# A hybrid attention, RG-LRU and conformer trunk whose own scheduler is given other durations for its matmuls

## The chip, the cores and the metric

The kernel runs on one core of a Trainium2 chip. The metric is the device time of one execution in microseconds (us). The core's engines are TensorE (PE in the profile; its weight loads are shown apart as PEld), VectorE (DVE), ScalarE (ACT), GpSimd (POOL) and SyncE (SP), which here only issues transfers (DMAs).

## The reference

Two layers of this, for 256 tokens of width 1024, all in float32 (cut; `causal_dwconv`, `banded_causal_attention` and the norms are left out):

```python
h = rms_norm(x, norm_mix_pre[l])
proj = h @ w_in[l]
q, k, v, lru_x, lru_gate, glu_in, gate_logits = jnp.split(proj, IN_SPLITS, axis=-1)
y_a = dilated_attention_mixer(q, k, v, cos, sin, w_o_attn[l])   # 3 groups of 8 heads of 64
y_b = rg_lru_mixer(lru_x, lru_gate, ...)                        # causal conv, gates, associative scan
y_c = conformer_conv_mixer(glu_in, ...)   # GLU, 31-tap causal conv, LayerNorm over 1024 channels
g = jax.nn.sigmoid(gate_logits).reshape(B, S, N_BRANCHES, D)
merged = g[:, :, 0] * y_a + g[:, :, 1] * y_b + g[:, :, 2] * y_c
x = x + rms_norm(merged @ w_out[l], norm_mix_post[l])
h = rms_norm(x, norm_mlp_pre[l])
u = jnp.square(jax.nn.relu(h @ w_mlp_up[l]))                    # 1024 -> 4096
x = x + rms_norm(u @ w_mlp_down[l], norm_mlp_post[l])
```

## The kernel before

**Weights.** The weight matrices come from HBM as 184 chunks of 128 x 2048 float32 (1 MB), each by one DMA that SP issues (tiles `raw_*`, two buffers). ACT casts each chunk to a shorter format (`whi_*`, two casts of 128 x 1024, line 416), DVE subtracts that from the chunk and keeps the rest (`wlo_*`, two subtractions, line 429), and PE multiplies in three passes: activations high and low (`hh`, `hl`) with `whi`, and activations high with `wlo`. A chunk gives 48 matmuls of 256 columns, or 24 of 512. They are the main matmuls. In names such as `wlo_gb1_1` the last digit is the layer (0 or 1); `q`, `k`, `v` are the attention's projections, `gb`, `ga`, `gc` the branch gates, `lx`, `lg`, `glu` the inputs of the other two branches, `ob` the output of the RG-LRU, `up` and `dn` the MLP.

**Beside the main matmuls** run: the rotary embedding on DVE (`r1q`, `r2q`, `r1k`, `r2k`); DMAs of 32 KB that copy its result, head by head, into `qk<head pair><group>`, eight per tile, four issued by SP and four by POOL; the scores `sc<head pair><token parity>` on PE, 12 float32 matmuls into the only `sc` buffer; two DVE reductions for each (`sm`, with the row maxima `mx`, line 969), the softmax on ACT, transposes (`tp`) and the products with v on PE; the 31 taps of the conformer conv, some as multiply-adds on DVE (`c`, 128 x 256, line 433), some as products on ACT (`cpd`, line 423) that DVE adds up in a tree of 1024, 512 and 256 columns (`cpd<-cpd`, line 429); the gates' merges (`mg`); the LayerNorm, whose sums over channels are float32 matmuls (`channel_sum`).

**The order.** The kernel doesn't write out its instructions in the order of the source. Each helper (`matmuls`, `tt`, `stt`, `act`, `dma`) makes an operation with an engine, a cost in ns, and what it reads and writes, and `Sched.run` plays a list schedule with these costs: whenever an engine is free in that play, it gets the ready operation with the longest path behind it, by the costs and a table of latencies. The order in which operations were given out is the order in which they are emitted, on all five queues. At run time each engine takes its queue strictly in that order and waits for semaphores, so that a wrong cost doesn't make an operation slow; it changes what stands ahead of what. The main matmuls are tied to each other in the sequence of the list `ORDER`

```python
ORDER = """
    v0 lx1 glu0 glu2 glu3 glu1 glu4 lx0 glu5 glu6 glu7 lx3 lx2 lw0 lw1 lw3 lg1 lg2 lw2 lg0 lg3 q10
    k00 k10 q00 q20 k20 gb0 ob0 gb2 gb1 q11 ob1 gb3 q01 ob3 ob2 ga1 k01 v2 k11 k21 q21 v1 ga0 ga2
    ga3 gc1 gc2 gc0 gc3 oa0 oa1 oc0 oc2 oc1 oc3
""".split()
```

so only the other PE work (scores, transposes, channel sums) can move between them, and so can everything on the other engines. A score operation needs the `sc` buffer free, that is both reductions of the score operation before.

Of the kernel before, what the change touches and what calls it, by code (L numbers as in the profile page):

```python
# [8 lines left out]
F32R = mybir.dt.float32r  # L9
# [367 lines left out]
def trunk_kernel(ctx: ExitStack, tc: tile.TileContext, x_d, pos_d, w_d, lruw_d, par_d, gain_d, const_d, id_d, out_d):  # L377
# [10 lines left out]
    def slot(name, dt=F32, shape=(P, 2, T)):  # L388
        return S.buf(sp, shape, dt, "s2", name, NSLOT)

    def mm_ps(name, shape=(P, 2, T), ring=True):
        return S.buf(pp, shape, F32, "mm", name, 4, ring)
# [4 lines left out]
    def stat(name):  # L397
        return S.buf(sp, (P, 1), F32, "st", name, 32)
# [12 lines left out]
    def act(out, in_, func, scale=1.0, bias=0.0, accum=None):  # L411
        cost = 0.833 * in_.n + (51 if in_.psum else 93) + 93 * aps(scale, bias) + (95 if accum else 0)

        def fn():
            if func is AF.Copy and not isinstance(scale, View) and scale == 1.0:
                nc.scalar.copy(out.ap(), in_.ap())  # L416
                return
            kw = {}
            if isinstance(bias, View) or bias != 0.0:
                kw["bias"] = val(bias)  # L420
            if accum is not None:
                kw["accum_out"] = accum.ap()
            nc.scalar.activation(out.ap(), in_.ap(), func, scale=val(scale), **kw)  # L423

        return S.op("ACT", cost, fn, [in_] + views(scale, bias), [out] + views(accum), TABLE.get(func))
# [19 lines left out]
    def recip(out, a):  # L445
        return S.op("DVE", 8.3 * out.n + 68, lambda: nc.vector.reciprocal(out=out.ap(), in_=a.ap()), [a], [out])

    def dma(eng, out, in_, nbytes):
        def fn():
            o = out.ap() if isinstance(out, View) else out  # L450
            i = in_.ap() if isinstance(in_, View) else in_
            eng.dma_start(out=o, in_=i)

        e = {id(nc.gpsimd): "POOL", id(nc.scalar): "ACT"}.get(id(eng), "SP")
        o = S.op(e, DMA_ISSUE[e], fn, views(in_), views(out))
        o.dma = nbytes / DMA_RATE / 1e3
        return o
# [4 lines left out]
    def matmuls(items):  # L462
        cost = 0
        reads, writes, seen = [], [], set()
        for out, lhs, rhs, start, stop in items:
            n = rhs.n
            cost += n * 0.4266 if lhs.buf.dt == F32R else n * 1.69
            for v, l in ((lhs, reads), (rhs, reads), (out, writes)):
                k = (id(v.buf), v.reg, l is writes)
                if k not in seen:  # L470
                    seen.add(k)
                    l.append(v)

        def fn():
            for out, lhs, rhs, start, stop in items:
                nc.tensor.matmul(out.ap(), lhsT=lhs.ap(), rhs=rhs.ap(), start=start, stop=stop)  # L476

        return S.op("PE", cost, fn, reads, writes)
# [10 lines left out]
    def main(items, *more):  # L489
        for it in (items,) + more:  # L490
            o = matmuls(it)
            o.main = True
            if last_main[0] is not None:
                S.follow(last_main[0], o)
            last_main[0] = o
        return o
# [146 lines left out]
    def add_residual(t, c, m, r):  # L643
# [5 lines left out]
    o = dma(nc.sync, x_sb[:, 0, :], x_d[0:P, :], D * P * 4)  # L649
# [3 lines left out]
                    2048 * P))  # L653
    g_rest = mm_ps("g_rest", (P, 512), False)
    matmuls([(g_rest.all(), unit[0:1, :], g_row[0:1, 512:1024], True, True)])
    S.follow(o, dma(nc.sync, ident.all(), id_d, P * P * 4))
    x1_load = dma(nc.sync, x_sb[:, 1, :], x_d[P:T, :], D * P * 4)
# [82 lines left out]
    for l in range(L):  # L740
# [212 lines left out]
        score_ops = []  # L953

        def scores(hp, t):
            ps = S.buf(pp, (P, 2, 512), F32, "sc", f"sc{hp}{t}_{l}", 1)
            own = slice(t, T, 2)
            it = []
            for g, c, n, ks in ((0, 0, 256, slice(0, T)), (1, 256, P, own), (2, 384, P, own)):
                for e in range(2):  # L960
                    q, rows = qk[hp, g], slice(64 * e, 64 * e + 64)
                    it.append((ps[:, e, c:c + n], q[rows, 0, own], q[rows, 1, ks], True, True))
            score_ops.append(matmuls(it))
            for e in range(2):
                hd = 2 * hp + e
                sb = S.buf(sp, (P, 512), F32, "sm", f"sm{hd}{t}_{l}", NSM)
                s = sb.all()
                mx, nm, ls, rl = (stat(f"{n}{hd}{t}_{l}") for n in ("mx", "nm", "ls", "rl"))
                S.op("DVE", 1.042 * 512 + 76, lambda s=s, mx=mx, e=e: nc.vector.tensor_tensor_reduce(
                    out=s.ap(), in0=ps[:, e, :].ap(), in1=mask[t].ap(), scale=1.0, scalar=-3.0e38, op0=OP.add,  # L970
                    op1=OP.max, accum_out=mx.all().ap()), [ps[:, e, :], mask[t]], [s, mx.all()])
                S.op("ACT", 94, lambda mx=mx, nm=nm: nc.scalar.mul(nm.all().ap(), mx.all().ap(), -0.125),
                     [mx.all()], [nm.all()])
                act(s, s, AF.Exp, scale=0.125, bias=nm.all(), accum=ls.all())
                recip(rl.all(), ls.all())
                act(s, s, AF.Copy, scale=rl.all())
                sm[hd, t] = sb
# [55 lines left out]
        def channel_sum(src, name):  # L1033
            part = mm_ps(f"{name}p_{l}", (P, T), False)
            for r in range(2):
                o = matmuls([(part[32 * c:32 * c + 32, :], ones[:, 0:32], src(4 * r + c), r == 0, r == 1)
                             for c in range(4)])
                o.cost *= 0.14
            sb = slot(f"{name}s_{l}", shape=(P, T))
            act(sb.all(), part.all(), AF.Copy, scale=1.0 / 32)  # L1040
            return sb

        def layer_norm():
            mu = mm_ps(f"mu_{l}", (P, T), False)
            matmuls([(mu.all(), ones.all(), channel_sum(lambda i: cacc[i // 2][:, i % 2, :], "mu").all(), True, True)])
            mub = mu.all().map(lambda a: a[:, None, :].to_broadcast([P, 2, T]))
            sqs = {}
            for j in range(4):
                tt(cacc[j].all(), cacc[j].all(), mub, OP.subtract)
                sqs[j] = slot(f"csq{j}_{l}")  # L1050
                act(sqs[j].all(), cacc[j].all(), AF.Square)
            vs = channel_sum(lambda i: sqs[i // 2][:, i % 2, :], "var")
            var = mm_ps(f"var_{l}", (P, 2), False)
            matmuls([(var[:, t:t + 1], vs[:, t * P:(t + 1) * P], ones[:, 0:1], True, True) for t in range(2)])
# [22 lines left out]
        def attention():  # L1077
            for hp in range(4):
                for t in range(2):
                    scores(hp, t)  # L1080
                for e in range(2):
                    for t in range(2):
                        p_transposes(2 * hp + e, t)
                pv(hp)
# [259 lines left out]
```

## Time and profile before

| what | value |
|---|---|
| median of 3 runs | 1123.21 us (1122.27, 1123.21, 1128.92) |
| the profiled execution | 1124.8 us |
| its span in the trace | 1123.0 us |
| mean granted clock of PE | 0.998 |
| PE busy | 1103.7 us, 98% of the span |
| PE weight loads busy | 1027.6 us, 92% |
| DVE, ACT, POOL busy | 903.7, 726.0, 70.8 us |

Costs are worked out in the trace of the profiled execution, whose own time is 1.6 us above the median; 1.8 us of it lie outside the span. A duration in the rows is that of one instruction from its start to its modelled end; several in a row overlap at their ends, so the step from one to the next is shorter than the duration.

### The profile page before, as it was taken

The numbers are of one execution on the slowest core, as the hardware profiler recorded it, in microseconds if no ns is written. First come the engines' busy times: TensorE is split into PE (matmuls) and PEld (weight loads), VectorE is DVE, ScalarE is ACT, GpSimd is POOL, SyncE is SP. The second block draws the span as 40 slices with busy tenths as digits, with TensorE's granted clock in tenths as the row PEclk, the third lists the DMA queues.
The fourth block names the chain that finished last, engine by engine and source line by source line (L and its number), as shares of the span: only waits on it lengthen the run. The fifth ranks groups of instructions, "written<-read, shape, count | busy, mean of one in ns | idle before, by whom it ended". The sixth has DMA issues, their size and how long they took to land.

```text
span 1123.0 us, 20583 instructions
## 1 busy us (share of the span) xinstructions
PE 1103.7 (98%) x8258; PEld 1027.6 (92%) x8258; DVE 903.7 (80%) x1380; ACT 726.0 (65%) x1184; POOL 70.8 (6%) x156
## 2 busy tenths in 40 slices
PE   7999998999999999999999999999999999999997
PEld 6999998999999889988889999989989998988996
DVE  6999999999969875555679999999997789655554
ACT  5879938588765554444569897469766656444443
POOL 1000021111000010000000000221200001000000
PEclk9999999999999999999999999999999999999999
DMA  8654365655255555555556553765634365655551
GB/s 293 245 208 151 146 219 205 215 165 174 99 186 188 214 199 189 208 193 182 201 188 205 190 179 121 255 216 170 214 124 151 117 240 185 212 192 185 190 203 52
DMA packets 37649, 209.76 MB, mean 187 GB/s; under 512 B 6449, under 2 KB 9777, under 8 KB 14130
## 3 DMA queue, kind: packets, MB, share of 16 engines
q1 hardware_dynamic: 32976, 200.05, 50.7%
q0 software_dynamic: 4576, 8.40, 2.2%
q8 instruction: 65, 1.06, 0.4%
q14 instruction: 30, 0.25, 0.1%
q10 hardware_dynamic: 2, 0.00, 0.0%
HBM read 201.08 MB, written 1.05 MB: 180 GB/s over the span
## 4 chain that ended last, share of the span: by engine, by line
PE 82%; DVE 9%; DMA 4%; ACT 3%; issue 1%; SPq 1%; DVEq 0%; POOL 0%; ACTq 0%
PE dn L476 15%; PE up L476 14%; PE glu L476 8%; PE v L476 5%; PE gc L476 4%; PE wo L476 4%; PE lx L476 4%; PE oc L476 4%; PE lg L476 4%; PE k L476 3%; PE ga L476 3%; PE ob L476 2%; PE ua L476 2%; PE oa L476 2%; PE gb L476 1%; DMA qk<-r1q 1%
## 5 line engine op out<-in xcount | busy, mean ns | idle before, releaser
L429 DVE TENSOR_TENSOR wlo_dn<-raw_dn,whi_dn 128x1024 fp32r<-128x1024 f32 (+1 forms) x66 | 75.8, 1190 | 68.4 <-ACT whi_dn L416 68.4
L416 ACT CAST whi_dn<-raw_dn 128x1024 fp32r<-128x1024 f32 (+1 forms) x66 | 64.4, 1022 | 75.6 <-PE dn L476 44.0
L433 DVE SCALAR_TENSOR_TENSOR c<-upad,parh,c 128x256 f32<-128x256 f32 x256 | 110.5, 479 | 0.1
L476 PE MATMUL up<-hh_mlp,whi_up 128*128 128x256 f32 x448 | 106.3, 278 | 0.0
L476 PE MATMUL up<-hl_mlp,whi_up 128*128 128x256 f32 x448 | 106.0, 278 | 0.0
L476 PE MATMUL dn<-wlo_dn,uh 128*128 128x512 f32 x256 | 100.5, 393 | 0.0
L476 PE MATMUL dn<-whi_dn,uh 128*128 128x512 f32 x256 | 100.4, 392 | 0.0
L429 DVE TENSOR_TENSOR wlo_up<-raw_up,whi_up 128x1024 fp32r<-128x1024 f32 x56 | 66.4, 1222 | 39.1 <-ACT whi_up L416 39.1
L423 ACT ACTIVATE cpd<-upad,parh 128x256 f32<-128x256 f32 x224 | 94.6, 500 | 4.1 <-DVE c L429 4.1
L476 PEld LDWEIGHTS up<-hl_mlp,whi_up 128*128 128x128 f32 x448 | 84.3, 188 | 0.6
L476 PEld LDWEIGHTS up<-hh_mlp,whi_up 128*128 128x128 f32 x448 | 84.2, 188 | 0.6
L416 ACT CAST whi_up<-raw_up 128x1024 fp32r<-128x1024 f32 x56 | 56.2, 1048 | 36.4 <-PE dn L476 17.4
L476 PE MATMUL dn<-whi_dn,ul 128*128 128x512 f32 x256 | 70.8, 392 | 0.0
L429 DVE TENSOR_TENSOR cpd<-cpd 128x1024 f32<-128x1024 f32 (+2 forms) x84 | 63.5, 775 | 0.9 <-ACT cpd L423 0.9
L476 PE MATMUL up<-hh_mlp,wlo_up 128*128 128x256 f32 x448 | 60.7, 278 | 0.0
L476 PE MATMUL glu<-hl_mix,whi_glu 128*128 128x256 f32 x256 | 59.6, 276 | 0.0
L476 PE MATMUL glu<-hh_mix,whi_glu 128*128 128x256 f32 x256 | 59.6, 276 | 0.0
L476 PEld LDWEIGHTS dn<-whi_dn,ul 128*128 128x128 f32 x256 | 48.0, 188 | 10.8
L476 PEld LDWEIGHTS dn<-wlo_dn,uh 128*128 128x128 f32 x256 | 48.0, 188 | 10.3
L476 PEld LDWEIGHTS dn<-whi_dn,uh 128*128 128x128 f32 x256 | 48.1, 188 | 10.3
L476 PEld LDWEIGHTS up<-hh_mlp,wlo_up 128*128 128x128 f32 x448 | 55.7, 188 | 0.0
L476 PEld LDWEIGHTS glu<-hl_mix,whi_glu 128*128 128x128 f32 x256 | 48.0, 188 | 0.0
(309 smaller groups left out, 3388.3 us busy)
## 6 DMA issues: line engine op xcount, KB each, us to landing
raw_dn<-w_in_stream SPq DMA_DIRECT2D x32, 1024.0 KB, 4.8
raw_up<-w_in_stream SPq DMA_DIRECT2D x28, 1024.0 KB, 4.8
raw_glu<-w_in_stream SPq DMA_DIRECT2D x16, 1024.0 KB, 4.9
raw_q<-w_in_stream SPq DMA_DIRECT2D x12, 1024.0 KB, 4.8
raw_k<-w_in_stream SPq DMA_DIRECT2D x12, 1024.0 KB, 4.8
raw_v<-w_in_stream SPq DMA_DIRECT2D x11, 1024.0 KB, 4.9
raw_lx<-w_in_stream SPq DMA_DIRECT2D x8, 1024.0 KB, 4.8
raw_lg<-w_in_stream SPq DMA_DIRECT2D x8, 1024.0 KB, 4.8
```

The lines of the kernel that those rows point to most:

```text
L416: nc.scalar.copy(out.ap(), in_.ap())
L423: nc.scalar.activation(out.ap(), in_.ap(), func, scale=val(scale), **kw)
L429: lambda: nc.vector.tensor_tensor(out=out.ap(), in0=a.ap(), in1=b.ap(), op=op), [a, b], [out])
L433: lambda: nc.vector.scalar_tensor_tensor(out=out.ap(), in0=a.ap(), scalar=val(s), in1=b.ap(), op0=op0, op1=op1), [a, b] + views(s), [out])
L476: nc.tensor.matmul(out.ap(), lhsT=lhs.ap(), rhs=rhs.ap(), start=start, stop=stop)
```

## The change

Three costs that the scheduler plays with are altered; nothing that is computed changes, only the order. A main matmul is taken as 0.446 ns a column where it was 0.4266. Float32 matmuls still cost 1.69 ns a column but at least 180 ns. An operation of the scores is then taken at 0.64 of the sum for its 12 matmuls, and an operation of the channel sums at 0.33 of it where it was 0.14. Below line 963 the changed kernel's lines stand one further down.

```diff
@@ -464,7 +464,7 @@ def matmuls(items):
         for out, lhs, rhs, start, stop in items:
             n = rhs.n
-            cost += n * 0.4266 if lhs.buf.dt == F32R else n * 1.69
+            cost += n * 0.446 if lhs.buf.dt == F32R else max(n * 1.69, 180)
@@ -961,6 +961,7 @@ def scores(hp, t):
             score_ops.append(matmuls(it))
+            score_ops[-1].cost *= 0.64
@@ -1035,7 +1036,7 @@ def channel_sum(src, name):
-                o.cost *= 0.14
+                o.cost *= 0.33
```

The sequence of the main matmuls is the same. On PE, counted in main matmuls of 256 columns, `sc00` keeps its place in both layers, `sc01` of layer 0 moves 24 later, `sc10` 96 earlier in layer 0 and 144 earlier in layer 1 (there it now stands 24 behind `sc01`, which keeps its place), the first transposes 72 to 128 earlier, and the LayerNorm's small products 16 to 232 earlier in layer 0 and up to 24 in layer 1.

DVE, layer 0, from the taps behind the low parts of `wlo_q11` to the second reduction of `sc00`. Before:

```order
L429 TENSOR_TENSOR cpd011_0_1152<-cpd011_0_1152 128x256
L429 TENSOR_TENSOR cpd002_0_1734<-cpd002_0_1734 128x256
L429 TENSOR_TENSOR c0_0_493<-c0_0_493,cpd011_0_1152 128x256
L429 TENSOR_TENSOR wlo_ob1_0_2248<-raw_ob1_0_2153,whi_ob1_0_2216 128x1024 x2
L429 TENSOR_TENSOR c0_0_493<-c0_0_493,cpd002_0_1734 128x256
L433 SCALAR_TENSOR_TENSOR c2_0_786<-upad4_0_85,parh_188,c2_0_786 128x256 x2
L969 ISA sm00_0_2280,mx00_0_2281<-sc00_0_2255,const_261 128x512
L969 ISA mx00_0_2281 128x1
L969 ISA sm10_0_2304,mx10_0_2305<-sc00_0_2255,const_261 128x512
```

After:

```order
L429 TENSOR_TENSOR cpd002_0_1678<-cpd002_0_1678 128x512
L429 TENSOR_TENSOR cpd012_0_1744<-cpd012_0_1744 128x512
L429 TENSOR_TENSOR cpd002_0_1678<-cpd002_0_1678 128x256
L429 TENSOR_TENSOR cpd012_0_1744<-cpd012_0_1744 128x256
L429 TENSOR_TENSOR c0_0_498<-c0_0_498,cpd002_0_1678 128x256
L429 TENSOR_TENSOR c0_0_498<-c0_0_498,cpd012_0_1744 128x256
L429 TENSOR_TENSOR wlo_ob1_0_2268<-raw_ob1_0_2154,whi_ob1_0_2234 128x1024 x2
L433 SCALAR_TENSOR_TENSOR c2_0_791<-upad4_0_85,parh_188,c2_0_791 128x256 x9
L970 ISA sm00_0_2337,mx00_0_2338<-sc00_0_2316,const_261 128x512
L970 ISA mx00_0_2338 128x1
L429 TENSOR_TENSOR wlo_gb3_0_2359<-raw_gb3_0_2229,whi_gb3_0_2323 128x1024 x2
L970 ISA sm10_0_2376,mx10_0_2377<-sc00_0_2316,const_261 128x512
```

Seven more multiply-adds (`c2`) and two tree additions of 512 columns stand ahead of the first reduction, and the two halves of `wlo_gb3` between the first and the second.

SP, layer 1, the transfers issued behind `raw_gb1`. Before:

```order
L452 DMA qk01_1_8282<-r1k10_1_8188 32x256 x2
L452 DMA qk00_1_8354<-r1k00_1_8147 32x256 x2
L452 DMA qk00_1_8354<-r1q00_1_8211 32x256 x2
L452 DMA raw_q11_1_8390<-w_in_stream 128x2048
L452 DMA qk02_1_8395<-r1q20_1_8226 32x256 x2
L452 DMA qk02_1_8395<-r1k20_1_8315 32x256 x2
L452 DMA raw_ob1_1_8433<-w_in_stream 128x2048
L452 DMA raw_gb3_1_8509<-w_in_stream 128x2048
```

After:

```order
L452 DMA qk01_1_8218<-r1k10_1_8170 32x256 x2
L452 DMA qk11_1_8241<-r1k10_1_8170 32x256
L452 DMA qk00_1_8280<-r1q00_1_8200 32x256 x2
L452 DMA qk11_1_8241<-r1k10_1_8170 32x256
L452 DMA raw_q11_1_8373<-w_in_stream 128x2048
L452 DMA qk10_1_8376<-r1k00_1_8136 32x256 x2
L452 DMA qk10_1_8376<-r1q00_1_8200 32x256 x2
L452 DMA raw_ob1_1_8432<-w_in_stream 128x2048
L452 DMA qk02_1_8451<-r1q20_1_8246 32x256 x2
L452 DMA qk02_1_8451<-r1k20_1_8322 32x256 x2
L452 DMA qk12_1_8481<-r1q20_1_8246 32x256 x2
L452 DMA raw_gb3_1_8512<-w_in_stream 128x2048
```

The copies of the second head pair (`qk11`, `qk10`, `qk12`) have moved up between those of the first, and `qk02`, which `sc00` reads, is now issued behind the 1 MB chunk `raw_ob1`. In layer 0 the same has happened.

DVE, layer 1, from the low parts of `wlo_q11` to the second reduction of `sc00`. Before:

```order
L429 TENSOR_TENSOR wlo_q11_1_8478<-raw_q11_1_8390,whi_q11_1_8463 128x1024 x2
L429 TENSOR_TENSOR c0_1_6779<-c0_1_6779,cpd012_1_7436 128x256
L433 SCALAR_TENSOR_TENSOR c2_1_7219<-upad4_1_2700,parh_188,c2_1_7219 128x256 x2
L429 TENSOR_TENSOR wlo_ob1_1_8530<-raw_ob1_1_8433,whi_ob1_1_8498 128x1024 x2
L433 SCALAR_TENSOR_TENSOR c2_1_7219<-upad4_1_2700,parh_188,c2_1_7219 128x256 x3
L969 ISA sm00_1_8562,mx00_1_8563<-sc00_1_8536,const_261 128x512
L969 ISA mx00_1_8563 128x1
L969 ISA sm10_1_8584,mx10_1_8585<-sc00_1_8536,const_261 128x512
```

After:

```order
L429 TENSOR_TENSOR wlo_q11_1_8475<-raw_q11_1_8373,whi_q11_1_8440 128x1024 x2
L433 SCALAR_TENSOR_TENSOR mg0_1_8509<-thgb0_1_8400,ob0_1_8378 128x512
L433 SCALAR_TENSOR_TENSOR c2_1_7085<-upad4_1_2582,parh_188,c2_1_7085 128x256 x6
L429 TENSOR_TENSOR wlo_ob1_1_8552<-raw_ob1_1_8432,whi_ob1_1_8521 128x1024 x2
L429 TENSOR_TENSOR cpd200_1_7914<-cpd200_1_7914 128x1024
L429 TENSOR_TENSOR cpd210_1_7990<-cpd210_1_7990 128x1024
L433 SCALAR_TENSOR_TENSOR c2_1_7085<-upad4_1_2582,parh_188,c2_1_7085 128x256 x3
L970 ISA sm00_1_8608,mx00_1_8609<-sc00_1_8587,const_261 128x512
L970 ISA mx00_1_8609 128x1
L970 ISA sm10_1_8611,mx10_1_8612<-sc00_1_8587,const_261 128x512
```

A merge (`mg0`) and four more `c2` stand ahead of `wlo_ob1`, and two tree additions of 1024 columns behind it, where one addition of 256 columns (`c0`) is gone.

## Rows read from the trace of the kernel before

**Rows 1.** The page: busy time by engine, and the granted clock in 40 slices.

```profile
PE 1103.7 (98%) x8258; PEld 1027.6 (92%) x8258; DVE 903.7 (80%) x1380; ACT 726.0 (65%) x1184; POOL 70.8 (6%) x156
...
PEclk9999999999999999999999999999999999999999
```

**Rows 2.** The chain in the MLP: start us, us, what.

```profile
443.85 10.90 PE up L476 x96
454.75 11.01 PE dn L476 x48
```

**Rows 3.** The waits of PE: us in total, times, longest us.

```profile
PE sc L476 <- DVE mx L969: 4.8, 2, 3.1
...
PE tp L483 <- ACT sm L423: 1.2, 1, 1.2
...
PE sc L476 <- DMA qk<-r1k: 0.5, 1, 0.5
```

**Rows 4.** The timeline of PE: start us, us, what, [idle before it <- releaser].

```profile
171.80 1.18 PE L476 MATMUL sc<-qk 64*128 64x256 f32 x12
...
179.04 1.82 PE L476 MATMUL sc<-qk 64*128 64x256 f32 x12 [3.15 <-DVE mx L969]
...
726.86 1.18 PE L476 MATMUL sc<-qk 64*128 64x256 f32 x12
...
732.60 0.83 PE L476 MATMUL sc<-qk 64*128 64x256 f32 x6 [1.64 <-DVE mx L969]
...
758.25 0.66 PE L483 MATMUL tp<-ident,sm 128*128 128x128 f32 x4 [1.18 <-ACT sm L423]
```

**Rows 5.** Windows: PE, PEld, DVE, ACT, POOL busy (instructions), PEclk, DMA share, GB/s.

```profile
176.00:180.00 4.00, 0.96 (x7) 0.97 (x9) 4.00 (x10) 4.00 (x9) 0.15 (x1) 0.92 0.65 227
180.00:184.00 4.00, 4.00 (x28) 3.78 (x26) 4.00 (x7) 4.00 (x10) 2.59 (x6) 0.65 0.60 154
184.00:188.00 4.00, 4.00 (x37) 4.00 (x36) 3.54 (x7) 3.79 (x9) 1.35 (x3) 1.00 0.72 283
...
728.00:732.00 4.00, 2.96 (x26) 2.76 (x24) 4.00 (x8) 4.00 (x10) 0.00 (x0) 1.00 0.77 254
```

**Rows 6.** The timeline of SP, layer 0.

```profile
163.37 1.15 SPq L452 DMA_DIRECT2D qk<-r1q  x2
...
166.45 0.34 SPq L452 DMA_DIRECT2D raw_ob<-w_in_stream  x1
```

**Rows 7.** The 32 KB copies from 130 to 215 us (a view by tile).

```profile
DMA to landing us min/median/max: 1.7/4.5/6.1
```

**Rows 8.** The chain in layer 1: the transfer that the next casts waited for.

```profile
720.32 6.19 DMA raw_ob<-w_in_stream
```

**Rows 9.** The waits of DVE from 100 to 165 us.

```profile
DVE wlo_gb L429 <- ACT whi_gb L416: 2.2, 2, 1.4
```

**Rows 10.** The timeline of DVE, layer 0.

```profile
174.19 2.36 DVE L429 TENSOR_TENSOR wlo_ob<-raw_ob,whi_ob 128x1024 fp32r<-128x1024 f32 x2 [1.01 <-ACT whi_ob L416]
...
178.81 0.08 DVE L969 DVE_READ_ACCUMULATOR2_ANT mx<- 128x1 f32 x1
...
189.54 2.06 DVE L433 SCALAR_TENSOR_TENSOR c<-upad,parh,c 128x256 f32<-128x256 f32 x5
```

**Rows 11.** The timeline of DVE, layer 1.

```profile
717.93 2.36 DVE L429 TENSOR_TENSOR wlo_gb<-raw_gb,whi_gb 128x1024 fp32r<-128x1024 f32 x2 [1.13 <-ACT whi_gb L416]
720.21 1.22 DVE L429 TENSOR_TENSOR cpd<-cpd 128x1024 f32<-128x1024 f32 x1
721.35 0.48 DVE L433 SCALAR_TENSOR_TENSOR c<-upad,parh,c 128x256 f32<-128x256 f32 x1
...
727.68 2.36 DVE L429 TENSOR_TENSOR wlo_ob<-raw_ob,whi_ob 128x1024 fp32r<-128x1024 f32 x2 [0.73 <-ACT whi_ob L416]
...
732.37 0.09 DVE L969 DVE_READ_ACCUMULATOR2_ANT mx<- 128x1 f32 x1
...
735.46 0.68 DVE L433 SCALAR_TENSOR_TENSOR mg<-thgb,ob 128x512 f32<-128x512 f32 x1
```

## The prediction

> **What bounds the kernel now.** I read the page first: PE is busy for 1103.7 of 1123.0 us, at the full granted clock in all 40 slices [rows 1]. Then the chain of waits, where the MLP shows the pace of undisturbed main matmuls: 96 of 256 columns in 10.90 us are 113 ns each, 48 of 512 in 11.01 us are 229 ns each [rows 2], so 0.443 to 0.448 ns a column. The change's 0.446 is that price; the old 0.4266 was 4% short. Third, the list of what PE waits for: 4.8 us in two waits of a score operation for the row maxima on DVE, 1.2 us of the first transposes for the softmax, 0.5 us of a score operation for a copied key [rows 3]; what else the list has is of the start and the first projection, where nothing moves. A better order can therefore win back 6.5 us, and what a slower clock behind a wait costs. That cost is in the windows: after 3.15 us of waiting in layer 0 [rows 4] the granted clock is 0.92 and then 0.65 (the lower level, 1.2 GHz, for most of that window, 2.4 GHz for the rest), and PE issues 28 matmuls in 180 to 184 us where 37 fit at full clock; behind the 1.64 us wait of layer 1 [rows 4] the clock stays at 1.00 [rows 5]. Nine matmuls at 113 ns are 1.0 us. Both waits have one form. There is one score buffer; `sc01` can't start before both reductions of `sc00` are done, and these stand on DVE behind the low parts of `wlo_ob1`, which wait for ACT's cast of a chunk that has just landed [rows 10, 11].
>
> **The change part by part.** It removes and adds no instruction, and each row's price stays; I follow the queues of PE, DVE and SP through the places where PE waits, and add up what each wait becomes.
>
> Steps of DVE, which the sum needs: consecutive rows overlap by some 0.08 us (the addition of 1024 columns is shown as 1.22, and the next row starts 1.14 behind it [rows 11]). So 1.14 for an addition of 1024 columns, 2.28 for the two low parts of a chunk, 0.60 for the merge of 512 [rows 11], taken for an addition of 512 too, 0.40 for a multiply-add (five in 2.06 [rows 10]), and 0.33 for an addition of 256 columns, which is the line through 512 and 1024 put forth to 256.
>
> *sc00 waits for qk02, both layers.* Before, SP issued `qk02` ahead of `raw_ob1`, from 163.37 [rows 6]. Now its four copies of 0.58 us each stand behind `raw_ob1`, which went out at 166.45 [rows 6] because its buffer came free with `wlo_gb1`. So they are issued until 166.45 + 0.34 + 4 x 0.58 = 169.1, and a 32 KB copy behind a chunk lands 4.5 us later in the median, 6.1 at most [rows 7]: 173.6 to 175.2. The last four matmuls of `sc00`, which alone read `qk02`, are due 0.9 us after its start at 171.80 [rows 4], at 172.7. The wait is 0.9 to 2.5; if the copies went with the chunk's own stream and not behind it, it would be none. I take 1.5, bounds 0 and 3. In layer 1 `raw_ob1` goes out at 720.32 [rows 8], the copies until 723.0, landing from 727.5 against a due time of 726.86 + 0.9 = 727.8 [rows 4]; I take 0.5, bounds 0 and 2.5.
>
> *sc01, layer 0.* Against before, DVE does two additions of 512 columns, seven multiply-adds and the two halves of `wlo_gb3` more ahead of the second reduction: 1.2 + 2.8 + 2.3 = 6.3 us. It had 0.6 us less between `wlo_gb1` and there, which leaves 5.7, and 1.01 us of waiting in front of `wlo_ob1` [rows 10] fill up: 4.7. DVE also comes to `wlo_gb1` with 2.8 us more work behind it (taps that were moved up ahead of `q20`), but it waited 2.2 us for the casts of `gb0` and `gb1` in this stretch [rows 9], so 0 to 0.6 of that is left. The second maximum ends at 178.9 [rows 10] before, and at 183.6 to 184.2 now. PE comes to `sc01` later too: 179.04 - 3.15 = 175.9 before [rows 4], plus 24 main matmuls (2.7 us) and the 1.5 of `sc00`, 180.1. So a wait of 3.5 to 4.1 us takes the place of one of 3.15: +0.5. The slower clock behind it is paid as before.
>
> *sc10, layer 0.* The copies come earlier, so the 0.5 us wait for the key goes [rows 3]; next late are the reductions of `sc01`, which DVE ends at about 192.2 by the same sum, while PE is there at about 192.0. Between -0.5 and +1.5, I take -0.2.
>
> *sc01, layer 1.* From `wlo_q11` on, DVE does the merge, four multiply-adds and two additions of 1024 columns more and one of 256 less: 0.6 + 1.6 + 2.3 - 0.3 = 4.2 us; 0.1 less stands ahead of it, and the 0.73 us idle in front of `wlo_ob1` fill up [rows 11]. Of the 2.8 us that were moved up earlier, 0 to 1.2 are left after the idle 1.13 at `wlo_gb1` and less before it [rows 11]. The second maximum ends at 732.46 before [rows 11], now at 735.8 to 737.0. PE's due time hardly moves: 732.60 - 1.64 = 731.0 [rows 4], plus 0.5. The wait grows from 1.64 to 4.4 to 5.6 us, +3.4. Here the order was made for a score operation that the scheduler takes for longer than it is: its 12 matmuls cost it 0.64 x 3.46 = 2.2 us, and the trace shows 1.18 [rows 4].
>
> *The clock, layer 1.* A wait of 1.64 us left the clock alone, one of 3.15 didn't [rows 4, 5]. The new wait is longer than both, so I add the 1.0 us of layer 0, bounds 0 and 1.5. [...]
>
> *tp, layer 1.* The first transposes were 1.18 us late behind the softmax [rows 4]; their places move, and the softmax now has some 3 us to spare: -1.2.
>
> *q20, both layers.* Its second low half stands behind 2.4 us more of taps, and arrives within half a microsecond of its use. I take +0.3 in all, bounds 0 and 1.5. The other low and high parts in the neighbourhood come up to 9 us later in work, where they had 9 to 12 us to spare. The LayerNorm's sums and the later scores move by few matmuls in stretches without waits: 0, bounds -0.5 and +2.
>
> The sum: 1.5 + 0.5 + 0.5 - 0.2 + 3.4 + 1.0 - 1.2 + 0.3 = +5.8 us. Against the profiled execution's 1124.8 that is 1130.6; the median of the runs is 1.6 lower, so I predict 1129.0 us.
>
> **The rivals.** *The better price wins the waits back.* With 0.446 the schedule that is played is in step with the chip, so that what it places just in time is in time: the waits of rows 3 go, 6.5 us, and the 1.0 of the clock, and the time is 1115.7. For it speaks that the first transposes and the late key are such just-in-time losses; against it that the maxima, the largest part, move the wrong way in the very queue that sets them.
>
> *The moves cancel.* `qk02` lands in time in both layers, and PE's later arrival at `sc01` meets the reductions; what is left is +0.5 + 3.4 - 1.2 - 0.2 at most, and a little less of each. Within 2 us of before, 1123.
>
> *Slower by over 1%.* DVE, which is behind in the stretch from `q20` to `gb1`, makes PE wait for low parts: 2.8 us of taps were moved up ahead of `q20`, `k20` and `gb0`. If none of it is absorbed by idle time, PE loses 2.8 us in each layer there and a stretch at the slower clock behind it (1.0), and the score waits take their upper bounds (+3.0, +2.5, +1.0, +4.0, +1.5 with the clock, -1.2): 7.6 + 10.8 = 18 us at most, 1141; from about half of that on it is over 1%, 1135. The 2.2 us of idle time in layer 0 [rows 9] speak against it, and that q20's first half moves by only 0.4 us.
>
> *There is far more to win than the waits show.* If the 92% of the weight loads [rows 1] were the measure, 1123.0 - 1027.6 = 95 us would be open, and an order that packs PE better could give 2 or 3% of that span, 1095. The Trainium skill says so (Perfetto Trace Analysis, Identifying the Most-Contended Engine: PE's matmul busy share is a bad measure of the room, the share of the weight loads a better one). The trace speaks against it: in the MLP nothing waits, and a matmul still steps by 113 ns [rows 2]; no order changes this step.
>
> **How the numbers follow.** The forecast (1125 to 1134) has 0.48, the waits won back 0.20, the cancelling 0.17, slower by over 1% 0.13, the far larger gain 0.02. The range reaches from 1115, just under the waits won back, to 1136, where the bounds of the forecast's terms (3 + 2.5 + 1 + 4 + 1.5 + 1.5 and the -1.7 of what is won, 12 us) end. One per cent is 11.2 us, and about what a measurement of this kernel can tell from no change: below 1112.0 lies only a part of the large gain, 0.03; above 1134.4 most of the slow case and the end of the forecast, 0.15; between them 0.82.
>
> **What would show it.** In the trace after, the last matmuls of `sc00` wait for a `qk` copy from layer 0's 172.7 on; `sc01` of layer 0 waits 3.5 to 4.1 us for DVE's maximum, with the clock under 1.00 behind it; `sc01` of layer 1 waits over 4 us, and the window behind it shows a clock under 1.00 too; the transposes near 758 us wait no more, and the MLP keeps its 10.90 us for 96 matmuls. The prediction is wrong if `qk02` lands with its chunk, if ACT's casts come earlier than I carry over (they stand in another order as well, and I have moved DVE against its old waits only), or if PE waits for low parts of weights at `q20` and `k20`.

## The result, and the profile after

The changed kernel takes 1132.81 us (median of 7 runs, 1132.28 to 1134.98) against 1123.21 us (median of 7 runs of the kernel before on the same chip, 1121.44 to 1128.92): a ratio of 1.0084 [1.006 to 1.0107], so it is slower by 0.6 to 1.1%, some 9.5 us. The profiled execution spans 1131.0 us where it was 1123.0. Each ratio below is to runs of the kernel before beside it, and leaves out two slow executions, one of 1367.69 us among the five of the version that follows and one of 2230.17 us of the kernel before.

The page of the changed kernel, busy time and granted clock as in [rows 1]:

```profile
PE 1105.5 (98%) x8258; PEld 1027.1 (91%) x8258; DVE 902.6 (80%) x1380; ACT 725.9 (64%) x1184; POOL 69.3 (6%) x156
...
PEclk9999999999999999999999999999999999999999
```

PE is as busy as before, and so are the others. What was lost is waiting, and the list of PE's waits (us in total, times, longest us) says where, beside [rows 3]:

```profile
PE sc L476 <- DVE mx L970: 6.1, 2, 3.1
PE psi L476 <- ACT lu L423: 3.0, 2, 1.6
...
PE ua L476 <- DVE hl_mlp L429: 1.6, 2, 0.8
PE pt_mlp L483 <- DVE mgg_pm L433: 1.4, 2, 0.9
...
PE psr L476 <- ACT thr L423: 0.3, 1, 0.3
```

The wait of the transposes `tp` is gone, and the score operation waits for the maxima 1.3 us longer. But two new kinds have come that the kernel before didn't have: the small products of the RG-LRU's gates (`psr`, `psi`) wait for ACT, and the first transposes and matmuls of the MLP (`pt_mlp`, `ua`) wait for DVE. The timeline of PE has them in place, beside [rows 4]:

```profile
94.02 0.38 PE L476 MATMUL psi<-luh,lwh 128*128 128x256 f32 x1 [1.65 <-ACT lu L423]
...
175.15 0.84 PE L476 MATMUL sc<-qk 64*128 64x128 f32 x4 [0.31 <-DMA qk<-r1k]
184.72 1.88 PE L476 MATMUL sc<-qk 64*128 64x256 f32 x12 [3.09 <-DVE mx L970]
...
386.42 0.66 PE L483 MATMUL pt_mlp<-ident,mgg_pm 128*128 128x128 f32 x4 [0.90 <-DVE mgg_pm L433]
...
390.62 0.73 PE L476 MATMUL ua<-whi_ua,hl_mlp 128*128 128x512 f32 x2 [0.79 <-DVE hl_mlp L429]
...
652.52 0.39 PE L476 MATMUL psi<-luh,lwh 128*128 128x256 f32 x1 [1.34 <-ACT lu L423]
...
739.34 1.18 PE L476 MATMUL sc<-qk 64*128 64x256 f32 x12 [3.02 <-DVE mx L970]
```

To size each place I took the step from one start on PE to the next, and what it exceeds the pace by (113 ns for 256 columns). Behind the first projection, and counting the steps that exceed it by over some 0.13 us, this is 19 us before and 27 after, between 7 and 8 of the 8.0 us. The parts:

| place | before | after | change |
|---|---|---|---|
| gates' products, both layers | 0 | 1.81 + 0.44 + 1.51 | +3.8 |
| start of the MLP, both layers | 0 | 2.21 + 1.81 | +4.0 |
| `sc00` for `qk02`, layers 0 and 1 | 0, 0 | 0.47, 0 | +0.5 |
| `sc01` for the maxima, layers 0 and 1 | 3.31, 1.81 | 3.25, 3.19 | +1.3 |
| `sc10`, `tp` | 0.63, 1.34 | 0, 0 | -2.0 |
| `q20`, both layers | 0.23 + 0.29 | 0 | -0.5 |

So the scores, the transposes and `q20` together come out 0.7 us better, and the loss is at places which the prediction had set to nothing. How a gate's wait comes about is seen on ACT. Its timeline in layer 0 before:

```profile
87.78 1.72 ACT L423 ACTIVATE cpd<-upad,parh 128x256 f32<-128x256 f32 x4
89.39 0.62 ACT L416 CAST luh<-lu 128x512 fp32r<-128x512 f32 x1
...
90.90 1.03 ACT L423 ACTIVATE lu<-lx,par 128x256 f32<-128x256 f32 x2
```

and after:

```profile
90.99 0.62 ACT L416 CAST luh<-lu 128x512 fp32r<-128x512 f32 x1 [1.06 <-DVE lu L433]
91.52 1.04 ACT L416 CAST whi_lg<-raw_lg 128x1024 fp32r<-128x1024 f32 x1
...
92.94 1.02 ACT L423 ACTIVATE lu<-lx,par 128x256 f32<-128x256 f32 x2
```

ACT now stands at `luh` for 1.06 us, since DVE isn't ready, where four products of taps had filled the time, and then casts a chunk first. The next `lu`, which frees the PSUM buffer that `psi` needs, comes 2.0 us later. At the start of the MLP it is DVE. Its timeline before, where the low part `hl_mlp` goes ahead of the second half of a chunk:

```profile
385.45 0.69 DVE L429 TENSOR_TENSOR hl_mlp<-pt_mlp,hh_mlp 128x512 fp32r<-128x512 f32 x1 [0.15 <-ACT hh_mlp L416]
386.05 1.22 DVE L429 TENSOR_TENSOR wlo_ua<-raw_ua,whi_ua 128x1024 fp32r<-128x1024 f32 x1
```

and after, where both halves go ahead of it, and PE waits:

```profile
387.61 2.35 DVE L429 TENSOR_TENSOR wlo_ua<-raw_ua,whi_ua 128x1024 fp32r<-128x1024 f32 x2
389.88 0.68 DVE L429 TENSOR_TENSOR hl_mlp<-pt_mlp,hh_mlp 128x512 fp32r<-128x512 f32 x1
```

The windows around the two waits of `sc01` (columns as in [rows 5]) show the clock:

```profile
180.00:184.00 4.00, 1.63 (x15) 1.43 (x13) 4.00 (x8) 4.00 (x8) 0.00 (x0) 1.00 0.41 174
184.00:188.00 4.00, 3.28 (x19) 3.06 (x20) 4.00 (x8) 4.00 (x12) 0.00 (x0) 0.62 0.74 246
...
736.00:740.00 4.00, 0.98 (x10) 0.81 (x11) 4.00 (x9) 3.26 (x5) 0.00 (x0) 1.00 0.55 231
740.00:744.00 4.00, 4.00 (x40) 3.72 (x38) 4.00 (x9) 2.57 (x10) 0.00 (x0) 1.00 0.38 111
```

In layer 0 it falls as before; in layer 1 a wait of nearly the same length leaves it at 1.00. This is one execution, and of the seven the one with the highest mean granted clock (0.997, the others 0.991 to 0.996): in the others PE was at the lower clock for longer, at places that no trace here shows. The chain in the MLP keeps the pace of [rows 2]:

```profile
447.49 10.89 PE up L476 x96
```

### The profile page after: what moved, and what is told of

Read it like the earlier page. It is cut to its first block, busy times and chain, and to the rows that moved or that the text cites. A ratio compares the mean times of both kernels' runs of the same rounds, so it can differ in the third digit from the quotient of the medians.

```text
span 1131.0 us, 20586 instructions
## 1 busy us (share of the span) xinstructions
PE 1105.5 (98%) x8258; PEld 1027.1 (91%) x8258; DVE 902.6 (80%) x1380; ACT 725.9 (64%) x1184; POOL 69.3 (6%) x156
## 3 DMA queue, kind: packets, MB, share of 16 engines
q8 instruction: 65, 1.06, 0.4%
## 4 chain that ended last, share of the span: by engine, by line
PE 73%; DVE 16%; DMA 6%; ACT 3%; issue 2%; SPq 0%; DVEq 0%; POOL 0%; ACTq 0%
PE dn L476 15%; PE up L476 14%; PE v L476 5%; PE q L476 4%; PE k L476 4%; PE ga L476 4%; PE lg L476 4%; PE glu L476 4%; PE gc L476 4%; PE ob L476 3%; PE ua L476 2%; DVE wlo_glu L429 2%; PE lx L476 1%; PE sc L476 1%; DMA raw_ob<-w_in_stream 1%
## 5 line engine op out<-in xcount | busy, mean ns | idle before, releaser
L476 PEld LDWEIGHTS dn<-whi_dn,ul 128*128 128x128 f32 x256 | 48.0, 188 | 10.8
```

## The experiments

Two theories stood against each other. **Theory 1**: the loss is made at the scores, by their new price (0.64) and the late `qk02`. **Theory 2**: it is the price of the main matmuls itself. At 0.4266, PE is played 4% too fast, so all that feeds it is ordered early; at 0.446, PE is played as it is, and that margin is gone. A step in the working of theory 2 is what the scheduler's own plan says against the trace: start on the chip minus planned start, in us, for operations of layer 0.

```
          PE: v01   lx2   psr0  q10   q20   sc00    DVE: wlo_v01  wlo_lx2  wlo_lg2  wlo_q10  wlo_q20  wlo_ob1
before       +2.2  +4.7  +4.9  +6.5  +7.2  +8.8         +2.2     +4.0     +4.7     +5.3     +8.7     +12.5
after        +2.1  +1.7  +1.6  +4.3  +4.1  +3.9         +2.3     +3.7     +3.7     +4.2     +6.4      +9.5
```

Before, PE drifts against its plan by some 0.2 us a chunk, (0.446 - 0.4266) ns x 48 x 256, and at `lx2` and `psr0` it is later than its feeders on DVE are. After, PE is 1.7 us late there and the feeders 3.7: what the plan puts just in time comes 2 us late. At the scores the feeders are 5.6 us later against their plan than PE, where it was 3.7 before.

**The main price alone** (on the kernel before):

```diff
-            cost += n * 0.4266 if lhs.buf.dt == F32R else n * 1.69
+            cost += n * 0.446 if lhs.buf.dt == F32R else n * 1.69
```

> Only the main matmuls' price is changed (0.446), the scores, the float32 floor and the channel sums keep the old prices. Theory 1 (the time was lost at the scores, because they are priced at 0.64): the waits of sc01 go back to 3.15 and 1.64 us, and the time to 1123 to 1126 us. Theory 2 (the true price of the main matmuls takes away a margin: in the play PE ran 4% too fast, so all that feeds it was ordered early; now it comes just in time, and late where another engine's price is too low): all of the loss is here, 1130 to 1135 us, with PE waits at the recurrent gates of both layers (3.0 to 4 us together) and at the start of both MLPs (3 to 4 us together).

Measured: 1133.54 us, ratio to before 1.0096 [1.007, 1.0121]. Its waits of PE (columns as above):

```profile
PE sc L476 <- DVE mx L969: 8.2, 3, 4.0
...
PE psi L476 <- ACT lu L423: 2.3, 2, 1.3
```

The main price does the whole of the loss without the others, and that speaks for theory 2. But the loss lies elsewhere than theory 2 had it. The waits at the start of the MLP, which it had put down to this price, are not there, and those at the gates come to 2.6 us with 0.3 at `psr`, below the 3.0 to 4 expected. In their place are longer waits at `sc01`, with a granted clock behind them at or near the half in both layers (window, columns as above); in the two windows that follow it is still 0.68 and 0.63:

```profile
184.00:188.00 4.00, 3.73 (x20) 3.42 (x21) 4.00 (x8) 3.08 (x7) 0.00 (x0) 0.50 0.73 262
...
740.00:744.00 4.00, 1.96 (x12) 1.70 (x12) 4.00 (x10) 2.07 (x7) 0.00 (x0) 0.51 0.37 109
```

Beside the kernel before, the waits behind the first projection grow by 4.3 us (10.8 against 6.5) and the span by 7.7 (1130.7 against 1123.0); most of the rest is PE's slower steps at the lower clock.

**The rest alone**: the whole change, but the main price as it was.

```diff
-            cost += n * 0.446 if lhs.buf.dt == F32R else max(n * 1.69, 180)
+            cost += n * 0.4266 if lhs.buf.dt == F32R else max(n * 1.69, 180)
```

> The main matmuls keep 0.4266; the scores, the floor and the channel sums are changed. Theory 1: part of the loss is here, 1126 to 1130 us. Theory 2: no loss, and as the first transposes now stand 72 main matmuls later, their 1.2 us wait in layer 1 is gone: 1121 to 1124 us.

Measured: 1122.01 us, 0.9978 [0.9963, 0.9994], and of the score waits 3.2 us are left:

```profile
PE sc L476 <- DVE mx L970: 3.2, 2, 2.0
```

Neither `tp`, nor the gates, nor the MLP wait; `oa`, which hadn't waited before, waits 1.2 us for its weights. Theory 1 falls: the new prices of the scores and sums don't cost time but save about 0.2%.

**The old price for the matmuls of the output projection and the MLP only** (on the changed kernel), which gives the start of the MLP its old order back:

```diff
-            cost += n * 0.446 if lhs.buf.dt == F32R else max(n * 1.69, 180)
+            cost += n * (0.4266 if out.buf.name[:2] in ("wo", "ua", "up", "dn") else 0.446) if lhs.buf.dt == F32R else max(n * 1.69, 180)
```

> The changed kernel, but the matmuls of the output projection and the MLP keep 0.4266, which gives back the old order at the start of both MLPs and nothing else of weight. Theory 2: the waits there (1.06 + 0.95 + 0.20 in layer 0, 0.65 + 0.96 + 0.20 in layer 1) go, 1128 to 1130 us. Theory 1, or if a wait there only stands in for one that comes behind it: 1132 to 1133 us as in the changed kernel.

Measured: 1129.40 us, 1.0053 [1.003, 1.0075]. The waits of `ua` and `pt_mlp` are gone, the others stay, and `sc01` waits up to 4.2 us:

```profile
PE sc L476 <- DVE mx L970: 7.0, 2, 4.2
PE psi L476 <- ACT lu L423: 2.9, 2, 1.6
```

Some 3.4 us of the median come back, near the 4.0 of the table, though layer 1 gives some away at its longer wait at `sc01` and behind it, where the clock falls to 0.73. The interval of this ratio overlaps that of the changed kernel, and so do those of the next two experiments: what tells these kernels apart is their lists, of one execution each.

**The old price for the early projections** (`v0`, `lx`, `glu`, the gates, `lg`; on the changed kernel):

```diff
-            cost += n * 0.446 if lhs.buf.dt == F32R else max(n * 1.69, 180)
+            cost += n * (0.4266 if out.buf.name[:2] in ("v0", "lx", "gl", "ps", "lg") else 0.446) if lhs.buf.dt == F32R else max(n * 1.69, 180)
```

> The changed kernel, but the main matmuls ahead of the first q (v0, lx, glu, the recurrent gates, lg) keep 0.4266. Theory 2: the gates' waits (3.8 us in both layers together) go; the waits at the MLP starts (4.0 us) stay, and at the scores PE leads by 4 us more, so sc01 waits less than 3 us: 1126 to 1130 us. Rival (the gates' waits only stand in for those behind them): 1131 to 1134 us.

Measured: 1129.55 us, 1.0059 [1.004, 1.0078]:

```profile
PE sc L476 <- DVE mx L970: 6.6, 2, 3.8
...
PE psi L476 <- ACT lu L423: 0.4, 1, 0.4
```

The gates' waits fall, as the list shows, from 3.0 to 0.4 us where the margin is given back, and the waits at the scores, around which the true price is kept, stay. So the margin works where it is given. There are two misses: the MLP has no waits at its start here either, though its price was left at 0.446, and the longest wait at `sc01` is 3.8 us where under 3 was expected. The execution in the trace is also the fastest of the five (1125.89 us, the others 1128.42 to 1129.92).

**The durations that the plan has wrong.** A scan on DVE (128 x 256) is played at 338 ns. In the trace of the kernel before, eight of them stand in a row, and the next row starts at 135.01, 4.67 us behind their start:

```profile
130.34 4.76 DVE L889 TENSOR_TENSOR_SCAN thi<-a,thi 128x256 f32<-128x256 f32 x8
```

So the step is 0.58 us, 582 ns for most of them, and the eight of a layer are played 2.0 us too short. This is the changed kernel with that price set right:

```diff
-                    S.op("DVE", 338, lambda av=av, bv=bv: nc.vector.tensor_tensor_scan(
+                    S.op("DVE", 582, lambda av=av, bv=bv: nc.vector.tensor_tensor_scan(
```

> The changed kernel, with the scans of the recurrence priced at 582 ns, as they take in the trace, and not 338: eight per layer, 2 us. Theory 1, in the form that DVE is played 2 us too early at the scores: the taps no longer stand ahead of the reductions, sc01 waits under 1.5 us in each layer, 1127 to 1130 us. Theory 2 says the same of the scores and that the gates and the MLP starts still cost their 7 to 8 us. If the taps ahead of the reductions are not what sets the wait, 1132 to 1133 us.

Measured: 1130.63 us, 1.0058 [1.0034, 1.0082]:

```profile
PE psi L476 <- ACT lu L423: 4.3, 2, 2.6
PE sc L476 <- DVE mx L970: 3.6, 3, 1.9
```

The waits at the scores, which come behind the scans, fall from 6.1 to 3.6 us; those at the gates, whose results the scans take, grow from 3.0 to 4.3. The longest wait at a score, 1.9 us, is still above the 1.5 expected. The same edit on the kernel before:

> The kernel before with one cost changed, the scans at 582 ns. On DVE the reductions move ahead of 1.1 us of taps in layer 0 and 0.8 us in layer 1, and the first transposes stand 48 main matmuls later. If the scans' cost is what sets the score waits, those fall by as much (3.15 to about 2.0, 1.64 to about 0.8 us), the 1.2 us of the transposes and the slow clock go: 1118 to 1120 us. If the scores' own price is needed for it as well: 1121 to 1124 us.

Measured: 1121.25 us, 0.9991 [0.9974, 1.0009], no difference that this can tell. That is the second branch of what was expected: the scores' own price is needed as well. Its list has 2.3 us for the maxima and 1.3 for a `qk` copy where [rows 3] have 4.8 and 0.5, and no `tp`.

**All of ACT and DVE made dearer in the same ratio** (on the changed kernel), so that PE and its feeders stand to each other as with the old price:

```diff
+        if eng in ("ACT", "DVE"):
+            o.cost *= 1.0455
```

> The changed kernel with its 0.446, but every cost of ACT and DVE in the play is raised by 4.55% too, so that PE stands to them as with 0.4266. Theory 2 (what counts is PE's lead over the engines that feed it, not the price itself): the waits at the gates and at the MLP starts go, 1120 to 1125 us. Rival (a price of 0.446 spoils the order in itself, by the transfers, whose prices are not scaled, or by where PE's own free work falls): 1130 to 1134 us.

Measured: 1124.73 us, 1.0022 [1.0004, 1.004]: with the true main price kept, 7 to 8 us of the loss come back.

```profile
PE psi L478 <- ACT lu L425: 2.9, 1, 2.9
...
PE sc L478 <- DVE mx L972: 2.3, 2, 1.4
```

The MLP's start waits for nothing. This tells the relation of the prices apart from the price itself, and in the time theory 2 holds. In the places it misses: those of `psi`, which were to go, are 2.9 us beside the changed kernel's 3.0, now all in layer 0, and `oa` waits 1.8. Nor is the relation all that counts: the rest alone, where it is the same, took 1122.0 us, with an interval that lies below this one. The prices of the transfers, and of PE's scores and transposes, weren't scaled here; which of them makes that difference no run tells. With the scan's price set right too:

> The kernel with 0.446 and all of ACT's and DVE's costs raised by 4.55%, and the scans at 582 ns raised likewise. Theory 2: its score waits (1.0 and 1.6 us) go and the rest stays, 1120 to 1123 us. Rival (PE leads by too much then, as with 0.41): 1127 us or more.

Measured: 1120.14 us, 0.9984 [0.9963, 1.0005]. No score operation waits any more; 1.2 us at `tp`, 1.0 at `psi` and some smaller waits are left.

**More margin still**: the rest alone with a main price of 0.41.

```diff
-            cost += n * 0.4266 if lhs.buf.dt == F32R else max(n * 1.69, 180)
+            cost += n * 0.41 if lhs.buf.dt == F32R else max(n * 1.69, 180)
```

> The run before with the old main price and the three other changes, but main matmuls at 0.41, 8% under what they take: PE leads by more still. Theory 2: no waits at the gates and the MLP starts, sc01 waits no longer than 2.2 and 1.3 us, 1119 to 1124 us. Rival (0.4266 is a lucky point between two ways of being late, and any move from it costs): 1126 us or more.

Measured: 1136.28 us, 1.0128 [1.0106, 1.015], the slowest of all, against theory 2's simple form:

```profile
PE q L476 <- DVE r2q L429: 3.0, 2, 2.5
PE oa L476 <- ACT whi_oa L416: 2.9, 2, 1.5
...
PE oa L476 <- DVE wlo_oa L429: 2.7, 2, 1.4
PE pv L476 <- ACT thga L423: 2.4, 1, 2.4
...
PE sc L476 <- DVE mx L970: 0.6, 1, 0.6
```

The scores wait for almost nothing, as the theory had it, but main matmuls of `q` and the products with v now wait for DVE and ACT at places that had no waits, and those of `oa` wait 5.6 us where the rest alone had 1.2. A margin helps up to a point only; what passes it was read from this list, and not isolated.

**The version that follows**: the rest alone, with the old main price as the margin, and the scan's true price.

```diff
-            cost += n * 0.446 if lhs.buf.dt == F32R else max(n * 1.69, 180)
+            cost += n * 0.4266 if lhs.buf.dt == F32R else max(n * 1.69, 180)
...
-                    S.op("DVE", 338, lambda av=av, bv=bv: nc.vector.tensor_tensor_scan(
+                    S.op("DVE", 582, lambda av=av, bv=bv: nc.vector.tensor_tensor_scan(
```

> The old main price, the three other changes, and the scans at their true 582 ns. If DVE's lead in the play at the scores sets the waits of sc01, they fall from 2.20 and 1.30 us to under 1 us each, 1119 to 1121 us; if not, 1121 to 1123 us as without it.

Measured: 1115.77 us, 0.9941 [0.9918, 0.9965]. The whole list of PE's waits:

```profile
PE pt_mix L483 <- DVE xn_mix L433: 2.8, 1, 2.8
PE g_rest L476 <- DMA g_row<-gain_in: 2.2, 1, 2.2
PE v L476 <- DVE wlo_v L429: 0.5, 1, 0.5
PE v L476 <- ACT hh_mix L416: 0.4, 1, 0.4
PE v L476 <- DVE hl_mix L429: 0.3, 1, 0.3
```

All of it is of the start and of the first projection; behind that PE waits for nothing in this execution. The time is below the 1119 to 1121 us expected. The same kernel once more, in more rounds and on another chip:

> The old main price with the three other changes and the scans at 582 ns, once more beside the run with the scans alone: 1115 to 1117 us again, and 2 to 4 us under the scans alone.

Measured: 1115.84 us, 0.9939 [0.9918, 0.996]. This time, in the same order, the scores and a gate do wait:

```profile
PE sc L476 <- DVE mx L970: 1.2, 2, 1.0
PE psi L476 <- ACT lu L423: 0.6, 1, 0.6
```

So a wait of this list can differ by a microsecond between two executions of one kernel, and smaller differences between the lists above say little. The gain over the scan's price alone is 5.4 us where 2 to 4 were expected. This kernel beats the one before by 0.4 to 0.8%, and the changed one by about 17 us (1132.8 - 1115.8, from different comparisons).

## Why the prediction was right in its sum and wrong in its places

The sign, the size (+5.8 forecast, +8.0 in the profiled spans, 9.5 in the medians) and the range held. But the terms didn't hold as they stood; the sum came out near because what I left out is of the same size as what I put too high. That is luck.

**The step that failed** is the first of the working: following the queues "through the places where PE waits". PE's price is that of every main matmul, so the order moves at places that had no waits too, and whatever was just in time there could start one. I set all of them to 0, with bounds of -0.5 to +2 that were thought for the LayerNorm's sums and the later scores. The gates and the MLP's start took 7.8 us. The rival "the better price wins the waits back" had the right lever with the wrong sign: a schedule in step with PE has no margin for feeders that are 2 us and more behind it.

**`sc00` and `qk02`**, forecast +1.5 and +0.5, measured 0.5 and 0. The copies landed at 174.3 to 175.3, just where I had them (173.6 to 175.2). The due time of 172.7 was wrong: PE came to `sc00` 2.1 us later than before (173.90 against 171.80 [rows 4]), by about its waits at the gates.

**`sc01`, layer 0**, forecast 3.5 to 4.1, measured 3.09. DVE's timeline carries the added work as I followed it:

```profile
175.16 2.36 DVE L429 TENSOR_TENSOR wlo_ob<-raw_ob,whi_ob 128x1024 fp32r<-128x1024 f32 x2 [0.53 <-ACT whi_ob L416]
177.44 3.65 DVE L433 SCALAR_TENSOR_TENSOR c<-upad,parh,c 128x256 f32<-128x256 f32 x9
...
184.50 0.07 DVE L970 DVE_READ_ACCUMULATOR2_ANT mx<- 128x1 f32 x1
```

The second maximum ends at 184.57, against 183.6 to 184.2 forecast; PE, due at 181.63 (184.72 - 3.09) and not at 180.1, takes more than that back.

**`sc01`, layer 1**, forecast 4.4 to 5.6, measured 3.02, so +1.4 in place of +3.4. PE's due time, which "hardly moves", moved by 5.4 us, from 731.0 to 736.3 (739.34 - 3.02), and DVE's second maximum by 6.7, from 732.46 [rows 11] to 739.19:

```profile
739.11 0.08 DVE L970 DVE_READ_ACCUMULATOR2_ANT mx<- 128x1 f32 x1
```

Of both, 3.6 us are layer 1's later start (its first matmuls of `v` are at 569.59 where they were at 565.95), which is no part of the sum. Within the layer DVE came 3.1 us later, where the sum had 3.4 to 4.5, and PE 1.7, where it had 0.5; the wait of 1.34 us at a gate is most of that. The wait at `sc01` grows by the difference: a PE that waits earlier gives its feeders time to catch up. I had also said that the scheduler takes a score operation for 2.2 us. That was wrong: its plan shows 1.73 us before and 1.11 after, and the trace 1.18 [rows 4]; no number of the sum hung on it.

**The clock, layer 1**, forecast +1.0, measured 0 in the profiled execution: the wait of 3.02 us left it at 1.00. The Trainium skill says that a kernel which waits too long for its data drops to the half clock and starts each piece of work cold (TensorE: Matmul & The Clock Gate, HAM oscillation). Layer 0 agrees, with 0.62 behind 3.09 us, and so do three of the experiments at their longest waits of `sc01` (4.0 us and a clock of 0.51 with the main price alone, 4.2 and 0.73 with the old price for the MLP, 3.8 and 0.52 with that for the early projections); layer 1 of this execution doesn't. The size was too low as well: the windows at 0.92 and 0.65 [rows 5] lack 0.43 x 4 = 1.7 us of clock, where counting matmuls in the second alone gave 1.0. And the 9s of the page's clock row [rows 1], read as the full clock, mean 90% or more: these windows lie in such a slice.

**`sc10`, `tp`, `q20`**, forecast -0.2, -1.2 and +0.3, measured -0.6, -1.3 and -0.5. The wait for the key and that for the softmax went as forecast; that of `q20`'s low half, which I feared would grow, went too.

**The other rivals.** The starving of low parts at `q20` and `k20` didn't come. The far larger room of 95 us didn't show: the version that follows, with at most some 2 us of waits behind the first projection, is at 1115.8 us, all but the time that I had given the case of the waits won back (1115.7), while its weight loads are busy for 92% of the span.

**What stays open.** Why the feeders are 3.7 us behind their plan from the first projections on isn't settled; the scans explain 2.0 us a layer of what comes later. That the old price serves as a margin rests on four kernels (the main price alone, the rest alone, the early projections, the scaled costs). But each is another order, and how many waits a given margin leaves isn't smooth: 0.41, 0.4266 and 0.446 give 1136.3, 1122.0 and 1132.8 us with the other prices new. A part of each difference may be the luck of one order, and no run varies the order at unchanged prices, which would size it; the waits at the MLP's start, which came with the changed kernel and neither with the main price alone nor with the early ones given back, are such a case.

## What to carry to other kernels

Where a scheduler plays durations to set an order, the truest price of the engine that bounds the kernel is not by that the best: here a price 4% short made it look hungry, and what feeds it was ordered with a margin for what the play has too short elsewhere, while 8% short was the worst. Set right the prices of the feeders first (here one scan, 338 against 582 ns: 6.2 us together with the scores' new price, nothing that could be told without it), and compare the starts in the trace with the planned ones engine by engine before touching the price of the bound. When a change of a cost table is to be predicted, look at the places that are just in time now, not only at those that wait.

## What the hardware did that I had not expected

The granted clock behind a wait didn't go by the wait's length alone. After a wait of 3.02 us in layer 1 of the changed kernel it stayed at 1.00, and so it did after 2.7 us in layer 0 with the old price for the early projections. After 3.09 us in layer 0 of the changed kernel it was 0.62 in the next window, and with the scan's price set right a wait at `sc01` of 1.9 us at most was followed by 0.57:

```profile
180.00:184.00 4.00, 4.00 (x26) 3.88 (x24) 4.00 (x9) 4.00 (x8) 2.37 (x5) 0.57 0.69 267
```

What else decides it no run here shows.
